# Feed-forward sums moved from POOL to DVE, and the next stage's first weights called for earlier

## The chip, the cores and the metric

The kernel runs on one core of a Trainium2 chip. The time is the device time of one execution, in microseconds (us); what is compared is the median of several executions. The engines are named as in the profile: PE (TensorE, matrix products; its weight loads are PEld), DVE (VectorE), ACT (ScalarE), POOL (GpSimd) and SP (SyncE, which issues most of the transfers from memory). Each engine runs its own instructions in order; a semaphore makes one wait for another.

## What is computed

A sequence of 512 tokens with 1024 features goes through two layers and a tail. Everything is in fp32.

```python
def _rmsnorm(x, gain):
    x32 = x.astype(jnp.float32)
    y = x32 * lax.rsqrt(jnp.mean(x32 * x32, axis=-1, keepdims=True) + NORM_EPS)
    return (y * gain).astype(x.dtype)

def _swiglu(x, w_gate, w_up, w_down):
    hid = jax.nn.silu(jnp.einsum('bsd,df->bsf', x, w_gate)) * jnp.einsum('bsd,df->bsf', x, w_up)
    return jnp.einsum('bsf,fd->bsd', hid, w_down)
```

Each of the two layers is a feed-forward stage (`ffn1`), a mixer (mLSTM, retention and gated delta side by side) and a second feed-forward stage (`ffn2`), each behind its own RMS norm and added to the residual stream `h`. The tail is a second mixer (a state-space part and a gated linear recurrence), a fifth feed-forward stage and a last norm. The change touches the five feed-forward stages, which are called here `ffn1_0`, `ffn2_0`, `ffn1_1`, `ffn2_1` and the last one.

## The kernel before, in words

**Data.** `h` is kept transposed, as eight tiles of 128 features by 512 tokens, `self.h[0]` to `self.h[7]` (in the order they are `h_77` to `h_84`). A product in fp32 is made of three: weight and input are both split in a high and a low half (ACT rounds the high half, DVE subtracts it to get the low half: `split` L260 and L261, `parts_of` L207 and L210), and PE adds high by high, high by low and low by high. A split weight of 1024 columns is `whi` and `wlo`; the parts of a quad are `wah/wal`, `wbh/wbl`, `wdh/wdl`.

**A feed-forward stage.** The gate and up weights are taken two by two: a *quad* is a block of 2 by 2 weight tiles, and one block of the output is made with seven products (named a to g) of sums of these weights with sums of the inputs, instead of eight. A quad with its seven products is called a pair here, as in the code; a gate pair and an up pair together give two tiles of hidden activations. A stage has 22 pairs, 20 of them loaded in full (100 in the kernel) and two from early weights. `load_quad` (L385 on) loads a quad: SP's `wsum` (L392), `wa` (L393) and `wrest` (L394), and a DMA issued by POOL that adds a second part of the quad into `wsum` in place (L395). `prepare` (L424 on) makes the weight sums that the seven products need, `wdh/wdl` from `ws = wsum + wrest` (L441), and the last ones from `wrest + ws` (L446). The sum at L441 is a POOL operation, kept in program order on POOL.

**The inputs.** `even` (L455 on) and `odd` (L473 on) make the input sums from two neighbouring tiles of `h`: `xe`, `xo` (scaled by the gain, on ACT), `n` and `t` (DVE), and their splits `bh/bl`, `nh/nl`, `th/tl`. `square` (L490) calls `squares` (L317): ACT squares a tile of `h` (L320), and POOL adds it to a running sum, each time into a new tile `sqa` (L324). The mixers and the last norm use `squares` too. `total` (L327) multiplies the sum with ones on PE to `nps` (L331), and `rsqrt` (L264) makes from it `R`, the scale of the norm, which is multiplied into the outputs of the products (`taken`, L511 on). So the products start before the norm is known.

**Order.** `items` writes out the order of a stage's products by hand; two are ahead of where their weights are made (`SPLITS` = 11 us of planned time) and loads twice as far (`LOADS` = 22). The instructions of each engine are then put in order by the Tile scheduler, by priorities and a model of time, within what the program allows. `wlo` of the sums for f and g, made from `wrest`, is the last to be ready in a pair.

**Early weights.** A stage's first two quads are loaded ahead in the stage before: `ahead` (L556) loads eight tiles `wr` (L406, 256 KB each) and makes their first sums `ws` (L409, DVE) and splits `weh/wel`. It is called by `nxt()`, a function that each stage is given: in `ffn` when it comes to the fifth of the last group's eight output products (`mm == 4`), in the first mixers at the third block of the output projection, in the second mixer at block 4. Before a mixer, `nxt()` only begins the stream of weights (`begin`, L226).

Of the kernel before, what the change touches and what calls it, by code (L numbers as in the profile page):

```python
# [11 lines left out]
AF = mybir.ActivationFunctionType  # L12
ALU = mybir.AluOpType
# [130 lines left out]
class Builder:  # L144
# [279 lines left out]
    def prepare(self, w, p):  # L424

        nc = self.nc
        if p in w.part:
            return
        if hasattr(w, "raw"):
            return self.prepare_early(w, p)  # L430
        lo, hi = slice(0, 512), slice(512, 1024)
        if p == "a":
            w.part["a"] = self.split(w.a11, "wa")
        elif p in "ce":
            t = self.parts_of(w.sums, late=True)
            w.part["e"], w.part["c"] = [x[:, lo] for x in t], [x[:, hi] for x in t]
        elif p == "b":
            w.part["b"] = self.split(w.rest[:, hi], "wb")
        elif p == "d":
            w.s2 = self.slot("ws")  # L440
            self.tc.keep_in_program_order(nc.gpsimd.tensor_tensor(w.s2, w.sums[:, lo], w.rest[:, lo], ALU.add))  # L441
            w.part["d"] = self.split(w.s2, "wd")
        else:
            self.prepare(w, "b")
            self.prepare(w, "d")
            nc.vector.tensor_tensor(w.rest[:, hi], w.rest[:, hi], w.s2, ALU.add)  # L446
            t = self.parts_of(w.rest)
            w.part["g"], w.part["f"] = [x[:, lo] for x in t], [x[:, hi] for x in t]
# [39 lines left out]
        self.split_to(tt, t)  # L488

    def square(self, v, k):  # L490
        v.acc = self.squares(k, v.acc)

    def matmuls(self, m, p, j, x, last):

# [75 lines left out]
    def ffn(self, gain, names, l, factor, nxt):  # L570
        nc = self.nc
# [8 lines left out]
        v = type("Normed", (), dict(gain=gain, xs=[], tmp={}, acc=None))  # L580
# [28 lines left out]
        sizes = [2 * (b - a) for a, b in zip((-1,) + ENDS, ENDS + (FB // 2 - 1,))]  # L609
# [7 lines left out]
        for c, it in enumerate(items):  # L617
            t = 0.0
            for d in range(c, len(items)):
                k, i, q = items[d][:3]  # L620
                if t > LOADS:
                    break
                if k == "p":
                    if pairs[i].w is None:
                        pairs[i].w = self.load_quad(pairs[i].key)
                    if t < SPLITS:
                        self.prepare(pairs[i].w, q)
                elif t < SPLITS:
                    for u in range(where[d] // UNIT, (where[d] + count(items[d]) - 1) // UNIT + 1):
                        self.load_unit(u)  # L630
                t += cost[d]
            if r is None and c >= (0 if start else 4):
                r = self.slot("R")
                self.rsqrt(r, self.total(v.acc), 1.0 / DM, self.slot)
                for m in pairs:
                    m.r = r
            if it[0] == "d":
                _, g, mm, ks, first, last = it
                if g == len(sizes) - 1 and mm == 4:
                    nxt()  # L640
                if first:
                    pds[mm] = self.ps("pd", tag=("mm", "mx")[mm % 2])
                self.mm3(pds[mm], (names[2], l, mm), (hids[g] if ks.stop is None else hids[g][:sizes[g] - 2])[ks if ks.stop is None else slice(None)], first=first, last=last)
                if last:
                    nc.vector.scalar_tensor_tensor(self.h[mm], pds[mm], factor, self.h[mm], ALU.mult, ALU.add)  # L645
                continue
            _, i, p = it
            m = pairs[i]
            self.product(m, p, v.xs)
            if p == "g" and i % 2 == 0:  # L650
                for o in m.o:
                    nc.scalar.activation(o, o, AF.Silu)
            elif p == "g":
                f = i // 2
                hid = hids[sum(f > e for e in ENDS)]
                for j, (g, u) in enumerate(zip(pairs[i - 1].o, m.o)):
                    nc.vector.tensor_tensor(g, g, u, ALU.mult)
                    hid.append((2 * f + j,) + self.split(g, "hid"))
# [98 lines left out]
    def mixer1(self, l, nxt):  # L757
        nc = self.nc
        if l == 0:
            self.ealog = self.const.tile([P, DEPTH + 1], F32, name="ealog")  # L760
            self.tc.keep_in_program_order(nc.scalar.activation(self.ealog, self.cols[:, COLS["alog"]:COLS["alog"] + DEPTH + 1], AF.Exp))
        xs, r, total = self.norm(f"mix_{l}")
        m = type("Mix", (), dict(l=l, xs=xs, r=r, y=[]))
        ps = self.proj(("small", l), xs)
        self.lockstep([self.rows1(m, ps), self.by_token(m, total), self.values(m)])
        self.queue = [self.retention(m), self.mlstm(m)]
        self.lockstep([self.delta(m, h) for h in range(GH)], STARTS, lambda i: int((i + 1) * RATE) - int(i * RATE))
        self.drain()
        for mm, pd in self.out_proj(("w_out", l), m.y, range(KB)):
            if mm == 2:  # L770
                nxt()
            nc.vector.tensor_tensor(self.h[mm], pd, self.h[mm], ALU.add)

    def out_proj(self, key, y, blocks, late=2, wave=4):
# [379 lines left out]
    def mixer2(self, after):  # L1154
        nc = self.nc
        xs, r, v, ps1 = self.norm_of_norm("final", "norm1")
# [15 lines left out]
        for g, d in enumerate(groups):  # L1172
            nxt = groups[g + 1] if g + 1 < SG else None
# [22 lines left out]
            nc.gpsimd.tensor_tensor(t, t, m.acc[j], ALU.add)  # L1196
            mix.append((j,) + self.split(t, "mix"))
        for j in range(KB):
            if j == 4:
                after()  # L1200
            ps = self.ps("pd")
            self.mm3(ps, ("w_out2", j), mix)
            nc.vector.scalar_tensor_tensor(self.h[j], ps, 0.5, self.h[j], ALU.mult, ALU.add)
# [456 lines left out]
```

## Time and profile before

| | us |
|---|---|
| median of 3 runs | 3453.12 (3452.86 to 3454.13) |
| the profiled execution, its own time | 3450.36 |
| its span, first to last instruction | 3448.2 |
| PE busy | 3197.3 (93%) |
| DVE busy | 2469.5 (72%) |
| ACT busy | 1557.1 (45%) |
| POOL busy | 663.4 (19%) |
| POOL, sums for d (L441), 100 | 161.0 |
| mean granted clock of PE | 0.971 |

The profile shows one execution. Its busy times say how much each engine had to do, its timeline when, and its waits which engine stood still and for whom. A line such as "PE pW L501 <- DVE wlo L210" says that PE stood still before a product at line 501 until DVE had finished a `wlo` at line 210. PE is the engine that is to be kept busy; idle time elsewhere matters only where PE waits for it in the end. The stages lie, by the first products of each, at about 0 (`ffn1_0`), 790 (`ffn2_0`), 1171 (`ffn1_1`), 1933 (`ffn2_1`) and 3077 us (the last).

### The profile page before, as it was taken

The numbers are of one execution on the slowest core, as the hardware profiler recorded it, in microseconds if no ns is written. First come the engines' busy times: TensorE is split into PE (matmuls) and PEld (weight loads), VectorE is DVE, ScalarE is ACT, GpSimd is POOL, SyncE is SP. The second block draws the span as 40 slices with busy tenths as digits, with TensorE's granted clock in tenths as the row PEclk, the third lists the DMA queues.
The fourth block names the chain that finished last, engine by engine and source line by source line (L and its number), as shares of the span: only waits on it lengthen the run. The fifth ranks groups of instructions, "written<-read, shape, count | busy, mean of one in ns | idle before, by whom it ended". The sixth has DMA issues, their size and how long they took to land.

```text
span 3448.2 us, 48282 instructions
## 1 busy us (share of the span) xinstructions
PE 3197.3 (93%) x18602; PEld 2755.7 (80%) x18602; DVE 2469.5 (72%) x4144; ACT 1557.1 (45%) x2607; POOL 663.4 (19%) x779
## 2 busy tenths in 40 slices
PE   5999999987999799999999799999999998999998
PEld 5988877777898698887777698887777777879887
DVE  6765778667685695677866686578788887568655
ACT  5443543335353453344334454355444366355334
POOL 2111124202111111112431211132111123121111
PEclk7999999998999899999999899999999999999999
DMA  5564222134554355433212346423333222345642
GB/s 147 137 169 133 84 94 75 45 98 109 145 138 129 113 139 155 135 95 101 72 55 70 108 132 162 132 80 107 92 97 105 83 80 79 116 124 140 163 132 79
DMA packets 142614, 383.53 MB, mean 111 GB/s; under 512 B 22320, under 2 KB 38832, under 8 KB 142384
## 3 DMA queue, kind: packets, MB, share of 16 engines
q1 hardware_dynamic: 127984, 328.02, 29.8%
q0 software_dynamic: 14400, 52.44, 9.5%
q8 instruction: 145, 2.38, 0.3%
q14 instruction: 85, 0.70, 0.1%
HBM read 376.99 MB, written 2.88 MB: 110 GB/s over the span
## 4 chain that ended last, share of the span: by engine, by line
PE 51%; DVE 24%; ACT 10%; issue 6%; DMA 5%; POOL 4%; SPq 0%; DVEq 0%; POOLq 0%; ACTq 0%
PE pd L248 7%; PE pd L250 7%; PE pd L249 7%; PE pX L501 7%; DVE wlo L210 6%; PE pW L501 3%; PE pj L250 3%; PE pj L249 3%; PE pj L248 3%; DMA wraw<-ws 2%; ACT whi L207 2%; DVE wbl L261 2%; PE pV L501 2%; DVE cacc L715 1%; DVE wrest L446 1%
## 5 line engine op out<-in xcount | busy, mean ns | idle before, releaser
L210 DVE TENSOR_TENSOR wlo<-wraw,whi 128x1024 fp32r<-128x1024 f32 x306 | 391.0, 1278 | 263.8 <-ACT whi L207 206.5
L207 ACT ACTIVATE whi<-wraw 128x1024 fp32r<-128x1024 f32 x306 | 322.4, 1054 | 461.0 <-DMA wraw<-ws 410.0
L249 PE MATMUL pd<-hidl,whi 128*128 128x512 f32 x880 | 347.0, 394 | 0.0
L250 PE MATMUL pd<-hidh,wlo 128*128 128x512 f32 x880 | 346.7, 394 | 0.0
L248 PE MATMUL pd<-hidh,whi 128*128 128x512 f32 x880 | 346.3, 394 | 0.0
L395 POOL DMA_DIRECT2D wsum<-wq x100 | 87.7, 877 | 1247.7 <-DMA wsum<-wq 902.5
L501 PE MATMUL pX<-tl,whi 128*128 128x256 f32 x800 | 224.7, 281 | 0.0
L501 PE MATMUL pX<-th,whi 128*128 128x256 f32 x800 | 224.7, 281 | 0.0
L501 PE MATMUL pX<-th,wlo 128*128 128x256 f32 x800 | 224.5, 281 | 0.0
L250 PE MATMUL pj<-x,wlo 128*128 128x512 f32 x476 | 191.8, 403 | 4.7 <-DVE wlo L210 4.7
L250 PEld LDWEIGHTS pd<-hidh,wlo 128*128 128x128 f32 x880 | 165.2, 188 | 38.6
L248 PEld LDWEIGHTS pd<-hidh,whi 128*128 128x128 f32 x880 | 165.3, 188 | 38.2
L249 PEld LDWEIGHTS pd<-hidl,whi 128*128 128x128 f32 x880 | 165.2, 188 | 38.0
L250 PE MATMUL pj<-xh,wlo 128*128 128x512 f32 x476 | 192.1, 404 | 3.3 <-DVE wlo L210 3.3
L248 PE MATMUL pj<-x,whi 128*128 128x512 f32 x476 | 192.6, 405 | 0.6 <-ACT whi L207 0.4
L248 PE MATMUL pj<-xh,whi 128*128 128x512 f32 x476 | 190.2, 400 | 3.1 <-ACT whi L207 3.1
L249 PE MATMUL pj<-x,whi 128*128 128x512 f32 x476 | 191.6, 403 | 0.0
L249 PE MATMUL pj<-xl,whi 128*128 128x512 f32 x476 | 189.3, 398 | 0.0
L441 POOL TENSOR_TENSOR ws<-wsum,wrest 128x512 f32<-128x512 f32 x100 | 161.0, 1610 | 119.4 <-DMA wsum<-wq 51.0
L645 DVE SCALAR_TENSOR_TENSOR h<-pd,h 128x512 f32<-128x512 f32 x120 | 82.4, 687 | 111.4 <-PE pd L250 111.3
L715 DVE SCALAR_TENSOR_TENSOR cacc<-cpad,cols,cacc 128x512 f32<-128x512 f32 x174 | 137.5, 790 | 28.0 <-ACT cacc L711 15.6
L501 PE MATMUL pW<-nh,wlo 128*128 128x256 f32 x400 | 117.2, 293 | 42.7 <-DVE wlo L210 42.7
(503 smaller groups left out, 9771.4 us busy)
## 6 DMA issues: line engine op xcount, KB each, us to landing
wraw<-ws SPq DMA_DIRECT2D x306, 512.0 KB
wsum<-wq SPq DMA_DIRECT2D x100, 512.0 KB
wrest<-wq SPq DMA_DIRECT2D x100, 512.0 KB
wsum<-wq POOLq DMA_DIRECT2D x100, 512.0 KB, 6.2
wa<-wq SPq DMA_DIRECT2D x100, 256.0 KB
wr<-wq SPq DMA_DIRECT2D x40, 256.0 KB
csb<-drow SPq DMA_DIRECT2D x32, 256.0 KB
bc<-drow SPq DMA_DIRECT2D x24, 256.0 KB
```

The lines of the kernel that those rows point to most:

```text
L207: ins = self.nc.scalar.activation(hi, src, AF.Copy)
L210: self.nc.vector.tensor_tensor(lo, src, hi.bitcast(F32), ALU.subtract)
L248: nc.tensor.matmul(ps, lhsT=wh, rhs=xh, start=st, stop=False)
L249: nc.tensor.matmul(ps, lhsT=wh, rhs=xl, start=False, stop=False)
L250: nc.tensor.matmul(ps, lhsT=wl, rhs=xh, start=False, stop=en)
L261: self.nc.vector.tensor_tensor(lo, src, hi.bitcast(F32), ALU.subtract)
L395: nc.gpsimd.dma_start(w.sums, src[:, 512:1536], accum_op=ALU.add)
L441: self.tc.keep_in_program_order(nc.gpsimd.tensor_tensor(w.s2, w.sums[:, lo], w.rest[:, lo], ALU.add))
L446: nc.vector.tensor_tensor(w.rest[:, hi], w.rest[:, hi], w.s2, ALU.add)
L501: self.nc.tensor.matmul(m.ps[bank][:, 0:HT], lhsT=a[:, j * P:(j + 1) * P], rhs=b, start=p in "acb" and j + i == 0, stop=last and i == 2, s ...
L645: nc.vector.scalar_tensor_tensor(self.h[mm], pds[mm], factor, self.h[mm], ALU.mult, ALU.add)
L715: nc.vector.scalar_tensor_tensor(acc, x[:, 1 + j:1 + j + S], w(j), acc, ALU.mult, ALU.add)
```

## The change

Three things are changed. The sum `ws = wsum + wrest` for product d is issued to DVE instead of POOL (it keeps its place in program order, now on DVE). In the feed-forward stages the running sum of squares is added on DVE, in place into the first square's tile, instead of on POOL into new tiles; the norms of the mixers and the last norm keep `squares`. And `nxt()` is called earlier: in `ffn` before the first output product of the last group, in the first mixers before the output projection, in the second mixer at block 1.

```diff
--- before.py
+++ after.py
@@ -438,7 +438,7 @@
             w.part["b"] = self.split(w.rest[:, hi], "wb")
         elif p == "d":
             w.s2 = self.slot("ws")
-            self.tc.keep_in_program_order(nc.gpsimd.tensor_tensor(w.s2, w.sums[:, lo], w.rest[:, lo], ALU.add))
+            self.tc.keep_in_program_order(nc.vector.tensor_tensor(w.s2, w.sums[:, lo], w.rest[:, lo], ALU.add))
             w.part["d"] = self.split(w.s2, "wd")
         else:
             self.prepare(w, "b")
@@ -488,7 +488,13 @@
         self.split_to(tt, t)
 
     def square(self, v, k):
-        v.acc = self.squares(k, v.acc)
+
+        sq = self.slot("sq")
+        self.nc.scalar.activation(sq, self.h[k], AF.Square)
+        if v.acc is None:
+            v.acc = sq
+        else:
+            self.nc.vector.tensor_tensor(v.acc, v.acc, sq, ALU.add)
 
     def matmuls(self, m, p, j, x, last):
 
@@ -636,7 +642,7 @@
                     m.r = r
             if it[0] == "d":
                 _, g, mm, ks, first, last = it
-                if g == len(sizes) - 1 and mm == 4:
+                if g == len(sizes) - 1 and mm == 0 and first:
                     nxt()
                 if first:
                     pds[mm] = self.ps("pd", tag=("mm", "mx")[mm % 2])
@@ -766,9 +772,8 @@
         self.queue = [self.retention(m), self.mlstm(m)]
         self.lockstep([self.delta(m, h) for h in range(GH)], STARTS, lambda i: int((i + 1) * RATE) - int(i * RATE))
         self.drain()
+        nxt()
         for mm, pd in self.out_proj(("w_out", l), m.y, range(KB)):
-            if mm == 2:
-                nxt()
             nc.vector.tensor_tensor(self.h[mm], pd, self.h[mm], ALU.add)
 
     def out_proj(self, key, y, blocks, late=2, wave=4):
@@ -1196,7 +1201,7 @@
             nc.gpsimd.tensor_tensor(t, t, m.acc[j], ALU.add)
             mix.append((j,) + self.split(t, "mix"))
         for j in range(KB):
-            if j == 4:
+            if j == 1:
                 after()
             ps = self.ps("pd")
             self.mm3(ps, ("w_out2", j), mix)
```

100 + 35 additions leave POOL and come to DVE; the other engines keep their instructions, in an order that differs locally. Three places show how.

The end of `ffn2_0`, on ACT, where the last output products' weights are split (`whi<-wraw`), the early weights of `ffn1_1` are split (`weh`), the hidden activations are split (`hidh`), and the first `h` of `ffn1_1` is scaled (`xe<-h_77`). Before:

```order
L652 ACTIVATE o<-o 128x512 x2
L207 ACTIVATE whi<-wraw 128x1024 x3
L260 ACTIVATE hidh<-o 128x512 x2
L207 ACTIVATE whi<-wraw 128x1024 x2
L260 ACTIVATE weh<-wr 128x512 x2
L260 ACTIVATE weh<-ws 128x512 x2
L466 ACTIVATE xe<-h_77,cols 128x512
L452 ACTIVATE bh<-xe 128x256
L452 ACTIVATE nh<-n 128x256
```

With the change:

```order
L658 ACTIVATE o<-o 128x512 x2
L207 ACTIVATE whi<-wraw 128x1024
L260 ACTIVATE weh<-wr 128x512 x2
L260 ACTIVATE weh<-ws 128x512
L207 ACTIVATE whi<-wraw 128x1024
L260 ACTIVATE weh<-ws 128x512
L260 ACTIVATE hidh<-o 128x512
L207 ACTIVATE whi<-wraw 128x1024
L260 ACTIVATE hidh<-o 128x512
L466 ACTIVATE xe<-h_77,cols 128x512
L207 ACTIVATE whi<-wraw 128x1024
L452 ACTIVATE bh<-xe 128x256
```

Two to four `whi<-wraw` and the `hidh` that stood ahead of the four `weh` now stand behind them, and `xe<-h_77` no longer waits for all of them. On SP the eight `wr` loads go out ahead of the last four `wraw` loads. At the ends of the mixers the orders show no such move.

The opening of `ffn2_0`, on DVE, from the last input sum `t` to `rv`, the first step of the norm's scale (`wel` and `ws` are early weights, `wal` and `wlo` belong to the first full quad). Before:

```order
L487 SCALAR_TENSOR_TENSOR t<-n,xo 128x256
L453 TENSOR_TENSOR tl<-t,th 128x512
L409 TENSOR_TENSOR ws<-wr 128x512
L261 TENSOR_TENSOR wel<-ws,weh 128x512
L261 TENSOR_TENSOR wal<-wa,wah 128x512
L409 TENSOR_TENSOR ws<-wr,ws 128x512
L210 TENSOR_TENSOR wlo<-wsum,whi 128x1024
L261 TENSOR_TENSOR wel<-ws,weh 128x512
L527 TENSOR_TENSOR oq<-pX,oq 128x256
L261 TENSOR_TENSOR wel<-wr,weh 128x512
L268 TENSOR_SCALAR rv<-nps 128x512
```

With the change:

```order
L487 SCALAR_TENSOR_TENSOR t<-n,xo 128x256
L453 TENSOR_TENSOR tl<-t,th 128x512
L409 TENSOR_TENSOR ws<-wr 128x512
L497 TENSOR_TENSOR sq<-sq 128x512
L261 TENSOR_TENSOR wel<-ws,weh 128x512
L261 TENSOR_TENSOR wal<-wa,wah 128x512
L409 TENSOR_TENSOR ws<-wr,ws 128x512
L210 TENSOR_TENSOR wlo<-wsum,whi 128x1024
L261 TENSOR_TENSOR wel<-ws,weh 128x512
L261 TENSOR_TENSOR wel<-wr,weh 128x512
L268 TENSOR_SCALAR rv<-nps 128x512
```

The last addition of squares, `sq<-sq`, now stands here between two steps of the early weights, and `oq<-pX,oq` comes after `rv`.

A pair of quads in the same stage, on DVE, from the low half of one sum to that of the next (`o` are outputs of products). Before:

```order
L210 TENSOR_TENSOR wlo<-wsum,whi 128x1024
L534 SCALAR_TENSOR_TENSOR o<-oq,R 128x256
L261 TENSOR_TENSOR wbl<-wrest,wbh 128x512
L522 TENSOR_TENSOR o<-pV,snap 128x256
L446 TENSOR_TENSOR wrest<-wrest,ws 128x512
L529 TENSOR_TENSOR o<-pW,snap 128x256
L261 TENSOR_TENSOR wdl<-ws,wdh 128x512
L530 TENSOR_TENSOR o<-o,R 128x512
L210 TENSOR_TENSOR wlo<-wrest,whi 128x1024
```

With the change:

```order
L210 TENSOR_TENSOR wlo<-wsum,whi 128x1024
L540 SCALAR_TENSOR_TENSOR o<-oq,R 128x256
L261 TENSOR_TENSOR wbl<-wrest,wbh 128x512
L528 TENSOR_TENSOR o<-pV,snap 128x256
L441 TENSOR_TENSOR ws<-wsum,wrest 128x512
L446 TENSOR_TENSOR wrest<-wrest,ws 128x512
L535 TENSOR_TENSOR o<-pW,snap 128x256
L261 TENSOR_TENSOR wdl<-ws,wdh 128x512
L536 TENSOR_TENSOR o<-o,R 128x512
L210 TENSOR_TENSOR wlo<-wrest,whi 128x1024
```

The sum `ws<-wsum,wrest` has come in behind `o<-pV,snap`, directly ahead of the addition that uses it.

## Rows read from the trace of the kernel before

**Rows 1.** The page: busy time of each engine, and the chain that ended last.

```profile
PE 3197.3 (93%) x18602; PEld 2755.7 (80%) x18602; DVE 2469.5 (72%) x4144; ACT 1557.1 (45%) x2607; POOL 663.4 (19%) x779
...
PE 51%; DVE 24%; ACT 10%; issue 6%; DMA 5%; POOL 4%; SPq 0%; DVEq 0%; POOLq 0%; ACTq 0%
```

**Rows 2.** Waits, whole span: waiter <- releaser: us in total, times, longest.

```profile
POOL ws L441 <- DMA wsum<-wq: 51.0, 12, 5.0
...
PE pW L501 <- DVE wlo L210: 42.7, 39, 2.4
...
DVE o L522 <- PE pV L501: 5.9, 14, 0.7
```

**Rows 3.** Groups by form, POOL then DVE: busy us, mean ns | idle before.

```profile
L441 POOL TENSOR_TENSOR ws<-wsum,wrest 128x512 f32<-128x512 f32 x100 | 161.0, 1610 | 119.4 <-DMA wsum<-wq 51.0 <-DVE R L274 32.8 <-DVE wel L261 10.4
...
L210 DVE TENSOR_TENSOR wlo<-wrest,whi 128x1024 fp32r<-128x1024 f32 x100 | 121.6, 1216 | 6.5 <-ACT whi L207 6.4
L261 DVE TENSOR_TENSOR wbl<-wrest,wbh 128x512 fp32r<-128x512 f32 x100 | 99.5, 995 | 41.2 <-ACT wbh L260 41.1
L446 DVE TENSOR_TENSOR wrest<-wrest,ws 128x512 f32<-128x512 f32 x100 | 84.5, 845 | 0.3
```

**Rows 4.** Tile `wbl`, its DVE line: duration in ns, minimum/median/maximum.

```profile
L261 DVE TENSOR_TENSOR wbl<-wrest,wbh x100: 675/685/2618, 74.3 to 3390.4; 128x512 fp32r<-128x512 f32 x100
```

**Rows 5.** Timeline, a pair late in `ffn2_0`: start, us, engine, operation [idle before].

```profile
1100.16 2.47 DVE L261 TENSOR_TENSOR wbl<-wrest,wbh 128x512 fp32r<-128x512 f32 x1 [1.03 <-ACT wbh L260]
...
1100.47 1.59 POOL L441 TENSOR_TENSOR ws<-wsum,wrest 128x512 f32<-128x512 f32 x1
...
1102.88 0.68 DVE L446 TENSOR_TENSOR wrest<-wrest,ws 128x512 f32<-128x512 f32 x1
...
1105.08 0.39 PE L501 MATMUL pW<-nh,wlo 128*128 128x256 f32 x1 [0.91 <-DVE wlo L210]
```

**Rows 6.** Timeline, opening of `ffn1_0`.

```profile
32.72 0.43 DVE L483 SCALAR_TENSOR_TENSOR n<-n,xo 128x256 f32<-128x256 f32 x1
...
36.38 0.75 DVE L522 TENSOR_TENSOR o<-pV,snap 128x256 f32<-128x256 f32 x2
...
38.20 9.69 POOL L324 TENSOR_TENSOR sqa<-sqa,sq 128x512 f32<-128x512 f32 x6
...
47.84 0.90 POOL L395 DMA_DIRECT2D wsum<-wq  x1
47.95 0.69 DVE L261 TENSOR_TENSOR wel<-ws,weh 128x512 fp32r<-128x512 f32 x1 [1.17 <-POOL sqa L324]
...
47.95 2.08 PE L331 MATMUL nps<-sqa,cst 128*128 128x512 f32 x2 [12.61 <-POOL sqa L324]
```

**Rows 7.** Timeline, opening of `ffn2_0`.

```profile
792.62 1.05 DVE L483 SCALAR_TENSOR_TENSOR n<-n,xo 128x256 f32<-128x256 f32 x1 [0.71 <-ACT xo L482]
...
806.90 2.08 PE L331 MATMUL nps<-sqa,cst 128*128 128x512 f32 x2 [4.60 <-POOL sqa L324]
...
813.85 1.69 POOL L441 TENSOR_TENSOR ws<-wsum,wrest 128x512 f32<-128x512 f32 x1 [1.30 <-DVE wal L261]
...
814.29 2.33 DVE L210 TENSOR_TENSOR wlo<-wsum,whi 128x1024 fp32r<-128x1024 f32 x1
...
824.87 0.38 PE L501 MATMUL pX<-th,weh 128*128 128x256 f32 x1 [2.73 <-ACT weh L260]
```

**Rows 8.** Timeline, end of `ffn2_0`; beginning of `ffn1_1`.

```profile
1139.92 1.06 ACT L207 ACTIVATE whi<-wraw 128x1024 fp32r<-128x1024 f32 x1 [2.84 <-DMA wraw<-ws]
...
1142.43 0.69 DVE L645 SCALAR_TENSOR_TENSOR h<-pd,h 128x512 f32<-128x512 f32 x1 [4.01 <-PE pd L250]
...
1151.67 0.71 ACT L466 ACTIVATE xe<-h,cols 128x512 f32<-128x512 f32 x1
```

**Rows 9.** Windows: busy us of each engine, granted clock, DMA share, GB/s.

```profile
60.00:390.00 330.00, 314.48 (x2177) 291.81 (x2177) 231.82 (x343) 147.71 (x235) 43.81 (x37) 0.99 0.50 133
1088.00:1105.50 17.50, 15.86 (x132) 15.44 (x131) 13.40 (x19) 8.44 (x14) 4.39 (x4) 1.00 0.70 157
```

## The prediction

> **What bounds the kernel now.** Four views were read, in this order. The page first: TensorE (PE) is busy 93% of the span and holds 51% of the chain that ended last; VectorE (DVE) is busy 72% and holds 24%; GpSimd (POOL) is busy 19% and holds 4% [rows 1]. So only time in which PE stands still can be won, and a part of that time is set by DVE. The waits come next: PE waits 39 times, 42.7 us in all, for `wlo`, the low half of a weight that DVE makes just before the products f [rows 2]. This is the repeated cost inside the feed-forward stages. The third view is the timeline of one such pair (a quad with its seven products). DVE's `wbl` starts at 1100.16, POOL's sum for d (L441) runs from 1100.47 to 1102.06, and `wbl` takes 2.47 us instead of its median 0.685 [rows 4, 5]. Behind it on DVE stand `o<-pV,snap`, `wrest<-wrest,ws` at 1102.88, ACT's `whi`, DVE's `wlo`, and PE starts late at 1105.08 after 0.91 us. The reader is to see that a POOL sum of 1.59 us costs DVE about as much as it costs POOL. The last view is the opening of a stage: PE waits 12.61 us in the first one and 4.60 us in `ffn2_0` for POOL's running sum of squares [rows 6, 7].
>
> **Part one: 100 sums for d go to DVE.** Removed from POOL: 100 operations of 1.61 us [rows 3]. Added to DVE: 100 operations of the same shape as `wrest`'s add and `wbl`, so 0.68 us each (the median of [rows 4]), 68 us in all, in a queue that is 232 of 330 us busy in such a stage [rows 9]. Given back: `wbl` averages 0.995 and `wrest`'s add 0.845 where 0.685 is the median of the shape, which is 31 + 16 = 47 us over 200 operations [rows 3, 4]; other operations that meet a sum (the `wlo` of 2.33 us in [rows 7] is one) come on top. DVE's total is thus about even, but the hold is not spread evenly: it sits in the pairs where PE waits. In the shown pair, without the hold, `wbl` ends at 1100.85, `o` at 1101.2, the new sum at 1101.9, and `wrest`'s add starts then instead of at 1102.88. That is 1.0 us earlier and covers the whole 0.91 us on PE. With the hold of that pair (1.8 us) less the added 0.68, the net is 1.1 us; with a smaller hold of 1.3 us it would be 0.6. I take 0.64 us for each of the 39 waits: **-25 us**. The bounds are -42.7 (all of the waits) and 0 (nothing, the rival below). The 61 pairs in which PE does not wait pay 0.68 us out of the time that DVE is idle; if that cover were gone they would cost 61 x 0.68 = 41 us. On POOL, the accumulating DMAs of later quads (L395) keep their order and lose a neighbour in the queue; nothing there gets later.
>
> The Trainium skill, page SBUF — State Buffer, section Who interferes with whom, says that a DVE operation with two SBUF inputs and a GpSimd operation that reads SBUF exclude each other, and that the one that starts first holds the shared interface while the other waits it out. The shown pair agrees with the full exclusion, but not with the order: `wbl` has the earlier start and was the one held. By the order rule alone the hold would not come from the sum, the steady gain would be 0, and the time that of rival C.
>
> **Part two: 35 adds of squares go to DVE.** In `ffn1_0` all eight squares come together. POOL's last six adds take 9.69 us, to 47.89, and PE's `nps` waits for them to 47.95 [rows 6]. On DVE, after `o` at 37.13, there now stand four adds, one weight sum, two adds, one `wel` and the last add: nine operations of 0.68, to 43.3. That is **-4.6 us**; bounds -6 (nothing held, closer spacing) and -2 (ACT's squares come later than DVE can use them). The DMA at 47.84 that stood behind the adds on POOL goes out earlier too.
>
> In the other four stages (`ffn2_0`, `ffn1_1`, `ffn2_1`, and the last one) each add follows its square as it comes. Two operations `n<-n,xo` in the interval are held, 1.05 us [rows 7] against 0.43 where POOL stands still [rows 6], so 1.2 come back. The last add takes 0.68 in place of POOL's 1.6 (9.69 / 6), but one weight sum of 0.68 stands ahead of it now: -0.2. The inserted adds stand behind `tl`, where DVE next waits for ACT; I charge 0.2 for them. That is -1.2 us for each start, **-4.8 us**; bounds -10 (the adds free, all holds gone, 2.4 each) and +5 (two adds of 0.68 in the way at each, nothing back). Then R, the scale of the norm: the `wlo` at 814.29 took 2.33 us under the sum at 813.85 [rows 7] where 1.22 is the mean of its form [rows 3]. `rv`, the first step of R, stands behind it; in the new order no sum for d stands ahead of `rv`. PE waits 2.73 us at 824.87 behind R [rows 7]. -1.1 us for each of four starts: **-4.4 us**, bounds -10.9 and 0.
>
> **Part three: the next stage's early weights.** The order shows that only one of the places really changes: the end of `ffn2_0`. Before, `xe`, the first operation of the next stage on ACT, runs at 1151.67 although its `h` is ready at 1143.1 [rows 8]: it stood behind four `weh` that waited for their weights. Now they stand ahead of the last four `whi<-wraw`. Up to 8 us of the ACT and DVE chain that PE waits for at the opening of `ffn1_1` can start earlier. I take **-5 us**: the queue of `whi<-wraw` between them takes some of it. Bounds -8 and +13: the eight loads of 256 KB now go out ahead of the last four weight loads, and 2.1 MB at the 157 GB/s of a full stretch are 13 us [rows 9]; the `whi` at 1139.92 waited 2.84 us for its load already, so there is no slack to hide it [rows 8]. I take the gain, because the last loads were queued early and PE has the earlier products to do. In the mixers the call moves, the queues do not: 0.
>
> **Sum.** -25 - 4.6 - 4.8 - 4.4 - 5 = -43.8 us against the profiled execution's own 3450.4, so 3406.6. The median of the runs shown is 2.8 us above that execution, hence **3409 us**.
>
> **Rivals.** (A) *DVE becomes the bound: slower.* The hold comes from something else, such as the descriptor work of L395, and the 0.68 us land on PE in every pair: +68 us, less the 18.8 of the openings and early weights, gives 3502. For it: DVE is the second engine of the chain [rows 1]. Against it: at 47.95 a `wel` runs 0.69 us under an L395, unheld [rows 6], and DVE waited for PE before `o<-pV` only 14 times, 5.9 us [rows 2], so DVE's own backlog is what the return shortens. It decides from 0.19 us per pair on (18.8 us over 100).
>
> (B) *The wait moves along.* POOL waited 12 times, 51.0 us, for quad loads before a sum [rows 2]. DVE is in order, so splits for PE now queue behind that wait. If all of it shows, 3460, at the edge of slower. Against it: `wrest`'s add stands right behind and needed the same sum.
>
> (C) *Nothing in the steady stages*: hold and added sum cancel. Only -18.8 remains: 3434. For it: 68 us added against 47 counted back. The Trainium skill, page Perfetto Trace Analysis, section Optimizing Scalar/DVE Operations, says the same of these two engines: as they share a read port, moving work from one to the other might not help. The pair in [rows 5] speaks against it.
>
> (D) *The early loads stall the end of `ffn2_0`*: +13 in place of -5, 3427.
>
> **How the numbers follow.** Forecast 0.60, C 0.15, D 0.11, A 0.08, B 0.06. Runs of this kernel tell 0.2% (7 us) from no change. The forecast, C and D are faster by more, less 0.03 for their upper tails: 0.83. B is half no change, half slower: with the tails 0.06 same; A and half of B: 0.11 slower. The range runs from 3380 (steady waits all gone and the openings near their lower bounds, about 70 us) to 3440 (C and some of its openings lost); A, B and the tails outside are just under 0.2.
>
> **What would show it.** Right: `wbl` near 0.69 and `wrest`'s add near 0.68 us on average; the wait of PE for `wlo` under 20 us; `nps` of the first stage near 43 us instead of 48; POOL near 450 us busy (663 less 161 for the sums and some 50 for the adds); DVE's busy time within 20 us of before. Wrong: DVE 60 us busier with `wlo` waits of PE at 40 or more (A or C), DVE waiting for `wsum` loads ahead of splits (B), or ACT's `whi<-wraw` waiting over 6 us near 1140 (D).

## The result, and the profile after

The changed kernel takes 3367.0 us (median of 4 runs, 3364.3 to 3370.8) where the kernel before takes 3453.0: a ratio of 0.9751, 95% interval 0.9735 to 0.9768, 86 us less. The direction was forecast; the size was not, and the range of 3380 to 3440 does not hold it.

The page of the changed kernel, its busy times and its chain, against [rows 1]:

```profile
PE 3177.6 (94%) x18602; PEld 2745.7 (82%) x18602; DVE 2438.4 (72%) x4279; ACT 1554.5 (46%) x2607; POOL 471.4 (14%) x644
...
PE 66%; DVE 17%; ACT 8%; issue 4%; POOL 3%; DMA 2%; SPq 0%; DVEq 0%; ACTq 0%; POOLq 0%
```

PE has the same 18602 products and holds 66% of the chain instead of 51%; DVE's share falls from 24% to 17%, though DVE has 135 operations more. Its busy time is 31 us less: 92 us of additions came (68.1 at L441, 24.1 at L497), so some 123 us of other time went. POOL is down to 471 us, near the 450 forecast.

The waits of PE that are now longest (waiter, releaser: us in all, times, longest):

```profile
PE pX L507 <- ACT bh L452: 23.4, 6, 5.5
PE pX L507 <- ACT weh L260: 20.7, 6, 8.5
PE nps L331 <- DVE sq L497: 14.0, 4, 3.8
```

The wait for `wlo`, 42.7 us and PE's longest before [rows 2], is 0.6 us now, and the one for the squares' sum, in all five stages together, 14.0. The groups of DVE by form, for [rows 3] and [rows 4]:

```profile
L210 DVE TENSOR_TENSOR wlo<-wrest,whi 128x1024 fp32r<-128x1024 f32 x100 | 121.7, 1217 | 0.0
...
L261 DVE TENSOR_TENSOR wbl<-wrest,wbh 128x512 fp32r<-128x512 f32 x100 | 68.6, 686 | 30.8 <-ACT wbh L260 30.8
...
L446 DVE TENSOR_TENSOR wrest<-wrest,ws 128x512 f32<-128x512 f32 x100 | 68.4, 684 | 0.3
...
L441 DVE TENSOR_TENSOR ws<-wsum,wrest 128x512 f32<-128x512 f32 x100 | 68.1, 681 | 0.0
...
L497 DVE TENSOR_TENSOR sq<-sq 128x512 f32<-128x512 f32 x35 | 24.1, 687 | 1.8 <-ACT sq L493 0.5
```

`wbl` and `wrest`'s add now average 686 and 684 ns, their length alone. They are not the only ones. Three more forms, in the kernel before:

```profile
L210 DVE TENSOR_TENSOR wlo<-wsum,whi 128x1024 fp32r<-128x1024 f32 x100 | 132.2, 1322 | 25.3 <-ACT whi L207 25.2
...
L530 DVE TENSOR_TENSOR o<-o,R 128x512 f32<-128x512 f32 x110 | 82.9, 753 | 0.7
...
L261 DVE TENSOR_TENSOR wal<-wa,wah 128x512 fp32r<-128x512 f32 x100 | 80.7, 807 | 22.5 <-ACT wah L260 22.0
```

and with the change:

```profile
L210 DVE TENSOR_TENSOR wlo<-wsum,whi 128x1024 fp32r<-128x1024 f32 x100 | 122.4, 1224 | 79.8 <-PE pd L249 47.0 <-ACT whi L207 17.4 <-ACT wbh L260 8.9
...
L536 DVE TENSOR_TENSOR o<-o,R 128x512 f32<-128x512 f32 x110 | 75.2, 683 | 0.2
...
L261 DVE TENSOR_TENSOR wal<-wa,wah 128x512 fp32r<-128x512 f32 x100 | 68.5, 685 | 7.8 <-ACT wah L260 7.1
```

A pair late in `ffn2_0`, DVE alone, for [rows 5]:

```profile
1071.78 0.69 DVE L261 TENSOR_TENSOR wbl<-wrest,wbh 128x512 fp32r<-128x512 f32 x1 [0.90 <-ACT wbh L260]
1072.38 0.42 DVE L528 TENSOR_TENSOR o<-pV,snap 128x256 f32<-128x256 f32 x1
1072.72 0.68 DVE L441 TENSOR_TENSOR ws<-wsum,wrest 128x512 f32<-128x512 f32 x1
1073.32 0.68 DVE L446 TENSOR_TENSOR wrest<-wrest,ws 128x512 f32<-128x512 f32 x1
1073.92 0.42 DVE L535 TENSOR_TENSOR o<-pW,snap 128x256 f32<-128x256 f32 x1
1074.59 1.23 DVE L210 TENSOR_TENSOR wlo<-wsum,whi 128x1024 fp32r<-128x1024 f32 x1 [0.25 <-PE pX L507]
1075.73 0.68 DVE L261 TENSOR_TENSOR wdl<-ws,wdh 128x512 fp32r<-128x512 f32 x1
1076.33 1.22 DVE L210 TENSOR_TENSOR wlo<-wrest,whi 128x1024 fp32r<-128x1024 f32 x1
```

`wbl`, `o`, the new sum and `wrest`'s add follow each other without a hole, as worked out ahead: 1.5 us from the start of `wbl` to that of `wrest`'s add, where it was 2.7. And the opening of `ffn1_0`, for [rows 6]:

```profile
36.40 0.75 DVE L528 TENSOR_TENSOR o<-pV,snap 128x256 f32<-128x256 f32 x2
...
37.07 2.27 DVE L497 TENSOR_TENSOR sq<-sq 128x512 f32<-128x512 f32 x3
39.86 0.69 DVE L497 TENSOR_TENSOR sq<-sq 128x512 f32<-128x512 f32 x1 [0.52 <-ACT sq L493]
...
40.51 0.87 POOL L395 DMA_DIRECT2D wsum<-wq  x1 [19.05 <-DMA wsum<-wq]
41.07 1.48 DVE L497 TENSOR_TENSOR sq<-sq 128x512 f32<-128x512 f32 x2
...
43.07 0.68 DVE L497 TENSOR_TENSOR sq<-sq 128x512 f32<-128x512 f32 x1
...
44.02 1.91 PE L331 MATMUL nps<-sq,cst 128*128 128x512 f32 x2
```

PE's `nps` starts at 44.02 instead of 47.95, and POOL's DMA, no longer behind the adds, at 40.51 instead of 47.84.

Where the 84 us between the two profiled spans (3448.2 and 3364.3) lie is read from two kinds of marks in each trace, the second `nps` product of a stage and the end of its last `h<-pd`. "Opening" is from the last `h` of the stage before to `nps`, "body" from there to the stage's own last `h`. Differences to the kernel before, in us:

| | openings, five in order | bodies, five in order | mixers | all |
|---|---|---|---|---|
| the change | -4.1, -2.4, -5.2, -2.8, -0.3 | -11.4, -13.6, -16.5, -15.0, -10.8 | -1.4 | -83.4 |
| only the 100 sums | +0.3, 0, 0, 0, +0.1 | -11.5, -10.2, -13.9, -12.0, -11.1 | -1.9 | -60.3 |
| only the squares | -4.2, -2.6, -1.5, -2.8, -0.3 | +3.0, +0.1, -1.9, -2.1, +3.7 | -4.4 | -12.9 |
| only the earlier weights | -0.1, 0, -3.6, 0, 0 | -0.1, +2.6, -2.6, -3.1, +2.9 | -4.2 | -8.1 |
| sums and squares | -4.3, -2.4, -1.3, -3.0, -0.8 | -10.3, -13.6, -16.8, -14.6, -11.4 | -7.9 | -86.1 |

A single execution differs from the next by a few us, above all in the mixers, so the last column is only good to that. Second profiles of the change and of sums and squares repeat the openings within 0.3 us and the bodies within 0.6 and 2.1. Where POOL's sums remain, the bodies can scatter more: with only the earlier weights the last stage, behind which there is nothing to load early, differs by 2.9.

### The profile page after: what moved, and what is told of

Its sections match the earlier page's. It is cut to its first block, busy times and chain, and to the rows that moved or that the text cites. A ratio compares the mean times of both kernels' runs of the same rounds, so it can differ in the third digit from the quotient of the medians.

```text
span 3364.3 us, 48101 instructions
## 1 busy us (share of the span) xinstructions
PE 3177.6 (94%) x18602; PEld 2745.7 (82%) x18602; DVE 2438.4 (72%) x4279; ACT 1554.5 (46%) x2607; POOL 471.4 (14%) x644
## 4 chain that ended last, share of the span: by engine, by line
PE 66%; DVE 17%; ACT 8%; issue 4%; POOL 3%; DMA 2%; SPq 0%; DVEq 0%; ACTq 0%; POOLq 0%
PE pX L507 15%; PE pd L250 8%; PE pd L248 8%; PE pd L249 8%; PE pW L507 7%; PE pV L507 4%; PE pj L250 3%; PE pj L249 3%; PE pj L248 3%; DVE wlo L210 3%; DVE cacc L721 1%; PE pt L678 1%; PE pt L679 1%; PE pt L680 1%; DMA bc<-drow 1%
## 5 line engine op out<-in xcount | busy, mean ns | idle before, releaser
L395 POOL DMA_DIRECT2D wsum<-wq x100 | 86.6, 866 | 1623.6 <-DMA wsum<-wq 1028.2
L210 DVE TENSOR_TENSOR wlo<-wsum,whi 128x1024 fp32r<-128x1024 f32 x100 | 122.4, 1224 | 79.8 <-PE pd L249 47.0
L507 PEld LDWEIGHTS pX<-th,whi 128*128 128x128 f32 x800 | 150.8, 189 | 3.5 <-DVE oq L533 3.5
```

The source lines that it names most:

```text
L210: self.nc.vector.tensor_tensor(lo, src, hi.bitcast(F32), ALU.subtract)
L395: nc.gpsimd.dma_start(w.sums, src[:, 512:1536], accum_op=ALU.add)
L507: self.nc.tensor.matmul(m.ps[bank][:, 0:HT], lhsT=a[:, j * P:(j + 1) * P], rhs=b, start=p in "acb" and j + i == 0, stop=last and i == 2, s ...
```

## The experiments

### The parts alone

Each of the three parts was made alone in the kernel before, and the first two together. Only the sums for d:

```diff
-            self.tc.keep_in_program_order(nc.gpsimd.tensor_tensor(w.s2, w.sums[:, lo], w.rest[:, lo], ALU.add))
+            self.tc.keep_in_program_order(nc.vector.tensor_tensor(w.s2, w.sums[:, lo], w.rest[:, lo], ALU.add))
```

> Only the 100 sums for d go to DVE. If nearly all of the steady gain is theirs: 3453 less some 62, 3391 (3385 to 3398), PE's waits for wlo at nearly 0, the openings as before (nps of the first stage near 48 us). Rival, that the steady stages gained through the squares or the earlier weights too (the whole order moved): 3410 to 3425, with half of the 42.7 us of waits still there.

Measured: 0.9831 of before (0.9816 to 0.9845), 58 us. The page of this kernel:

```profile
PE 3184.2 (94%) x18602; PEld 2751.8 (81%) x18602; DVE 2436.1 (72%) x4244; ACT 1556.2 (46%) x2607; POOL 522.2 (15%) x679
```

The waits of PE for `wlo` are 0.4 us in all, the openings stand as before. Five bodies give 10 to 14 us each. So the sums carry two thirds of the gain by themselves; the first theory holds.

Only the squares:

```diff
-        v.acc = self.squares(k, v.acc)
+        sq = self.slot("sq")
+        self.nc.scalar.activation(sq, self.h[k], AF.Square)
+        if v.acc is None:
+            v.acc = sq
+        else:
+            self.nc.vector.tensor_tensor(v.acc, v.acc, sq, ALU.add)
```

> Only the 35 adds of squares go to DVE. If the openings gain by themselves: 4 us in the first stage and about 2.5 us in each of ffn2_0, ffn1_1 and ffn2_1, nothing in the last: 3453 less 11, 3442 (3438 to 3446), waits for wlo still 40 us or more. Rival, that the openings gained because the sums for d had left POOL's queue: under 5 us, 3448 or more.

Measured: 0.9967 (0.9956 to 0.9978), 11 us. The openings gain what they gain in the whole change, the first 4.2 us and the next three 2.6, 1.5 and 2.8; only `ffn1_1` gains more in the whole change (5.2), and that is the third part. Two waits of PE in this kernel:

```profile
PE pW L507 <- DVE wlo L210: 41.6, 36, 2.7
...
PE nps L331 <- DVE sq L497: 13.9, 4, 3.8
```

The wait for `wlo` is still there, that for the squares is 13.9 us in the feed-forward stages (32.7 before, with those of the other norms). The openings gained by themselves.

Only the earlier call for weights:

```diff
-                if g == len(sizes) - 1 and mm == 4:
+                if g == len(sizes) - 1 and mm == 0 and first:
                     nxt()
...
+        nxt()
         for mm, pd in self.out_proj(("w_out", l), m.y, range(KB)):
-            if mm == 2:
-                nxt()
...
-            if j == 4:
+            if j == 1:
                 after()
```

> Only the earlier call for the next stage's weights. If it makes the second half of the gain at the opening of ffn1_1: -2 to -5 us there and nothing elsewhere, 3449 (3446 to 3452). Rival, that it does nothing that can be measured: 3452 to 3455. Rival, that the early loads delay the last products of ffn2_0: 3456 or more.

Measured: 0.9993 (0.9981 to 1.0005), no difference. ACT's timeline of this kernel, the row that was at 1151.67 [rows 8]:

```profile
1146.68 0.72 ACT L466 ACTIVATE xe<-h,cols 128x512 f32<-128x512 f32 x1 [3.43 <-DVE h L645]
```

`xe` is 5 us earlier, and now waits for its `h`, which is made 3.5 us later than before (1146.6 instead of 1143.1). The opening of `ffn1_1` gains 3.6 us. The 2.6 us that the body of `ffn2_0` has lost are not the price of it, for 2.1 of them were lost by the sixteenth `h<-pd`, at 1085.2, and the first early load is issued at 1118.8: the end of the stage, from there to its last `h<-pd`, takes 81.5 us instead of 81.0. So some 3 to 4 us are gained at one place, which the times of whole executions (2 us less, between 7 less and 2 more) cannot tell from nothing.

The first two parts together, without the third, ran twice, the second time on one chip with the changed kernel itself.

> The change without the earlier weights. If the parts add up: 3367 plus 2 to 5 us, 3371 (3368 to 3374). Rival, that the order of the stage ends matters more: 3378 or more.

> The changed kernel again, as the measure for the other three on the same chip: about 0.975 of before.

> The change without the earlier weights, on the chip on which the change itself runs. If the earlier weights only trade the end of ffn2_0 for the opening of ffn1_1: within 4 us of the changed kernel. Rival, that they give my 5 us: 4 to 8 us slower.

Measured: 0.9767 (0.9750 to 0.9784) at first; on the common chip 0.9756 (3368.4 us) against 0.9746 (3365.8 us) of the change, intervals that overlap. In the profiles the earlier weights show in one place, the opening of `ffn1_1`, which gains 5.2 us with them and 1.3 without; the body of `ffn2_0` gains 13.6 either way. The first two parts give 11 to 14 us more together than one by one (0.0233 and 0.0244 off, where 0.0169 and 0.0033 make 0.0202), though each of these is known only to some 5 us: in the table the bodies gain 67 us together, where the sums alone give 59 and the squares alone cost 3. A part of it is PE's wait for `th,weh` behind R: 10.8 us before, 9.9 with the sums, 8.0 with the squares, 5.6 with both. The 8 us that both gain over the sums alone lie at the beginning of the bodies: from `nps` to the first `h<-pd`, `ffn2_0`, `ffn1_1` and `ffn2_1` together take 310 us before and with the sums, 305 with the squares, 302 with both. The squares alone lose some 7 us in the rest of the bodies, about what bodies with sums on POOL scatter by. More than that is not explained.

### Hold or lateness

A sum on POOL could cost in two ways: it holds DVE while it runs, or it comes late, since it takes 1.6 us and stands in POOL's queue. Two kernels separate them. The first puts the load back on POOL without its result: to the changed kernel, 100 additions of constants in the old place, which nobody reads (`dz` is a spare tile).

```diff
             self.tc.keep_in_program_order(nc.vector.tensor_tensor(w.s2, w.sums[:, lo], w.rest[:, lo], ALU.add))
...
+            f = lambda i: self.cst[:, i:i + 4, :].rearrange("p a b -> p (a b)")
+            self.tc.keep_in_program_order(nc.gpsimd.tensor_tensor(self.dz, f(0), f(4), ALU.add))
```

> The changed kernel plus 100 additions of constants on POOL, of the same shape and in the old place of the sums in POOL's order, whose result nobody reads. If the cost of before was the hold of DVE by a running POOL sum: DVE's wbl and its neighbours average 0.8 us or more again, waits for wlo come back in part, 12 to 45 us slower than the changed kernel (3380 to 3412). Rival, that it was the late arrival of the sum (POOL's queue and its 1.61 us): no more than 5 us slower, 3372 or less.

Measured: 1.0016 of before (1.0005 to 1.0027), that is 3459 us: the whole gain of the change is gone, 91 us at 0.9751. The expectation for the hold named 12 to 45 us, so its direction came true and its size did not. Two waits of PE, the page, and three rows of the timeline of a pair:

```profile
PE pW L511 <- DVE wlo L210: 50.1, 47, 2.1
...
PE pX L511 <- DVE oq L537: 12.2, 8, 2.3
```

```profile
PE 3199.0 (93%) x18602; PEld 2755.0 (80%) x18602; DVE 2543.6 (74%) x4279; ACT 1554.3 (45%) x2607; POOL 612.3 (18%) x744
```

```profile
1007.44 1.60 POOL L445 TENSOR_TENSOR dz<-cst 128x512 f32<-128x512 f32 x1
...
1007.64 1.95 DVE L441 TENSOR_TENSOR ws<-wsum,wrest 128x512 f32<-128x512 f32 x1
...
1009.52 0.68 DVE L450 TENSOR_TENSOR wrest<-wrest,ws 128x512 f32<-128x512 f32 x1
```

DVE is busy 105 us more than in the changed kernel with the same operations. In the timeline the sum on DVE starts 0.2 us after POOL's addition and takes 1.95 us instead of 0.68; it ends 0.55 us after POOL's 1009.04. Nobody needs POOL's result, so lateness is out. The hold alone is enough.

Which operations are held can be counted in the trace of the kernel before. Of 118 DVE operations with both inputs in SBUF that run beside one of the 100 sums, 74 are more than 0.15 us longer than others of their form; of 38 with an input from PSUM (`o<-pV`, `o<-pW`, `oq<-pX` and such), none is longer by more than 0.02 us.

The second leaves the hold and takes the lateness away: in the kernel before, the sum stays on POOL and is issued a step earlier, with the split of `wsum`.

```diff
             t = self.parts_of(w.sums, late=True)
+            self.early_sum(w)
...
-            w.s2 = self.slot("ws")
-            self.tc.keep_in_program_order(nc.gpsimd.tensor_tensor(w.s2, w.sums[:, lo], w.rest[:, lo], ALU.add))
+            self.early_sum(w)
...
+    def early_sum(self, w):
+        if getattr(w, "s2", None) is None:
+            nc, lo = self.nc, slice(0, 512)
+            w.s2 = self.slot("ws")
+            self.tc.keep_in_program_order(nc.gpsimd.tensor_tensor(w.s2, w.sums[:, lo], w.rest[:, lo], ALU.add))
```

> The kernel before, with the sum for d still on POOL but issued one step earlier, when the sums for e and c are split. If the late arrival was the cost: the waits for wlo fall under 15 us and 30 to 55 us are won, 3392 to 3417. Rival, that the hold was the cost: it only meets other DVE operations, waits for wlo stay over 25 us, 3432 to 3450.

Measured: 0.9978 (0.9967 to 0.9990), 8 us. Three waits of PE, and two groups of DVE:

```profile
PE pX L507 <- ACT snap L523: 19.4, 23, 1.5
...
PE pW L507 <- DVE wlo L210: 12.6, 24, 1.5
PE pX L507 <- DVE oq L533: 12.2, 18, 1.0
```

```profile
L210 DVE TENSOR_TENSOR wlo<-wsum,whi 128x1024 fp32r<-128x1024 f32 x100 | 143.6, 1436 | 68.5 <-ACT whi L207 34.7 <-ACT wbh L260 33.9
...
L261 DVE TENSOR_TENSOR wbl<-wrest,wbh 128x512 fp32r<-128x512 f32 x100 | 83.4, 834 | 62.6 <-ACT wbh L260 58.9 <-DMA wa<-wq 3.6
```

The wait for `wlo` did fall to 12.6 us, as the lateness would have it, but PE now waits for `snap` (7.4 us before) and `oq` instead, and `wlo<-wsum` averages 1436 ns where its length alone is 1224. The hold has met other operations of the chain: DVE is busy 2458.3 us in all, only 11 less than before. The time, not the one wait, decides: the expectation of 3432 to 3450 for the hold is the one that holds, though not by the row that it named.

### What POOL has to do to hold DVE

> The changed kernel plus 100 writes of a constant on POOL (128x512, nothing read), where the additions of constants cost 92 us. If the hold comes from what POOL reads, as the Trainium skill, page SBUF - State Buffer, section Who interferes with whom, has it: within 8 us of the changed kernel (3367 to 3375). Rival, that any POOL work at that place holds DVE or delays POOL's transfers: 3390 or more.

Against the kernel with the additions of constants:

```diff
-            self.tc.keep_in_program_order(nc.gpsimd.tensor_tensor(self.dz, f(0), f(4), ALU.add))
+            self.tc.keep_in_program_order(nc.gpsimd.memset(self.dz, 1.0))
```

Measured: 3362.4 us, 0.9727 (0.9707 to 0.9746). That is no slower than the changed kernel (0.9735 to 0.9768 on another chip; the two intervals overlap). The group of the writes on POOL, and the page:

```profile
L444 POOL MEMSET dz<- 128x512 f32 x100 | 81.2, 812 | 0.9
```

```profile
PE 3172.6 (95%) x18602; PEld 2743.5 (82%) x18602; DVE 2439.3 (73%) x4279; ACT 1555.0 (46%) x2607; POOL 526.0 (16%) x744
```

100 writes of 0.81 us in the same place, and DVE's busy time is that of the changed kernel (2438.4): of the 154 operations with both inputs in SBUF that run beside a write, none is held by more than 0.01 us. Such work on POOL, its place and the delay of its transfers cost nothing that can be measured. The additions differ from the writes in that they read SBUF. The Trainium skill, page SBUF — State Buffer, section Who interferes with whom, says this: an operation of DVE with two SBUF inputs meets a GpSimd operation that reads, not one that only writes. The trace agrees: 105 us of DVE's time beside the additions against none beside the writes, and no hold where one of DVE's inputs came from PSUM.

> The changed kernel plus 100 additions of constants on POOL of half the width (128x256). If a hold first uses up the slack of its pair (about 0.4 us, as the 68 us of added DVE work that cost some 22 us say) and only the rest reaches PE: 10 to 35 us slower than the changed kernel, 3377 to 3402. Rival, that a hold costs in proportion to its length: half of 92, 3408 to 3418.

Again against the kernel with the additions of full width:

```diff
-            self.tc.keep_in_program_order(nc.gpsimd.tensor_tensor(self.dz, f(0), f(4), ALU.add))
+            self.tc.keep_in_program_order(nc.gpsimd.tensor_tensor(self.dz[:, lo.start:256], f(0)[:, 0:256], f(4)[:, 0:256], ALU.add))
```

Measured: 3401.0 us, 39 us above the kernel with the writes on the same chip. The page:

```profile
PE 3190.5 (94%) x18602; PEld 2750.7 (81%) x18602; DVE 2499.8 (74%) x4279; ACT 1553.6 (46%) x2607; POOL 556.7 (16%) x744
```

The additions of half width take 1.05 us each, little more than a write of a constant (0.81), and DVE is busy 61 us more than with the writes. So it is not the time that POOL is busy that holds DVE. 3401.0 us lies just inside the interval of the theory with a slack (3377 to 3402); by the kernel with the writes, on the same chip, the 39 us are just above its 35, and under the rival's half of 92. Per microsecond of DVE's added time it is 39 / 61 = 0.64 us, where the full width costs 91 / 105 = 0.87: the first part of a hold is cheaper than the rest.

### What an added sum on DVE costs

> The changed kernel plus a second addition (of constants, result unread) on DVE behind each sum: another 68 us of DVE work in the same place. If the added 0.68 us lie in DVE's slack, as the vanished waits say: at most 10 us slower, 3377 or less. Rival, that DVE was at its limit with the change (my 0.64 us per wait, half eaten by the added sum): waits for wlo come back with 20 us or more, 3387 to 3435.

```diff
             self.tc.keep_in_program_order(nc.vector.tensor_tensor(w.s2, w.sums[:, lo], w.rest[:, lo], ALU.add))
...
+            self.tc.keep_in_program_order(nc.vector.tensor_tensor(self.dz, f(0), f(4), ALU.add))
```

Measured: 3388.4 us, 0.9816 (0.9799 to 0.9834), 22 us above the change at 0.9751. The page, and the longest new wait of PE:

```profile
PE 3191.4 (94%) x18602; PEld 2749.2 (81%) x18602; DVE 2492.4 (73%) x4379; ACT 1552.6 (46%) x2607; POOL 471.2 (14%) x644
```

```profile
PE pX L511 <- DVE oq L537: 11.1, 26, 1.0
```

68 us more of DVE's work cost a third of that. Neither expectation holds whole: it is more than the 10 us of the first, and the time is at the lower edge of the rival's (3387 to 3435), but the waits for `wlo` are 4.3 us and not 20. With twice as much:

> The changed kernel plus two additions of constants on DVE behind each sum, 1.36 us per pair, about as long as a hold. If a hold costs what the DVE time in it costs, and the pair's slack is 0.4 us: about 0.9 us per pair, 70 to 105 us slower than the changed kernel. Rival, that DVE time behind the sum is cheaper than a hold and a hold does more than take DVE's time: 30 to 60 us slower.

```diff
+            self.tc.keep_in_program_order(nc.vector.tensor_tensor(self.dz, f(0), f(4), ALU.add))
+            self.tc.keep_in_program_order(nc.vector.tensor_tensor(self.dz, f(0), f(4), ALU.add))
```

Measured: 3433.9 us, 68 us above the changed kernel on the same chip (3365.8). That is a little under the first interval and above the second. The first 68 us of DVE's work cost 22, the next 68 cost 46: as if there were a slack in each pair that the first one uses up for the most part. But 136 us of it cost 68, while 105 us of holds cost 91. So a microsecond of hold is dearer than one of work behind the sum. A hold meets whichever operation comes, and some pairs not at all, which is a reason, but it was not tried with holds of equal length in every pair; this stays open.

### Attempts at a faster kernel

> The changed kernel with the norm's sum on PE two products later in four openings. If PE's 14 us of waits for nps are only its place in PE's order: 6 to 12 us faster than the changed kernel, 3355 to 3361. Rival, that the scale R then comes late and PE waits there: within 3 us or slower.

```diff
-            if r is None and c >= (0 if start else 4):
+            if r is None and c >= (0 if start else 6):
```

Measured: 3374.7 us, 0.9777 (0.9761 to 0.9793), no gain, rather some us lost. Waits of PE:

```profile
PE pW L507 <- ACT weh L260: 29.8, 11, 7.5
PE pV L507 <- ACT weh L260: 16.9, 5, 4.7
...
PE nps L331 <- DVE sq L497: 10.0, 4, 3.1
```

`nps` is waited for 10.0 instead of 14.0 us; the products that now stand ahead of it wait for their `weh` instead, 29.8 us where `pW` waited 11.2. `nps` starts no earlier and no later than in the change, and from there to the first `h<-pd` it is some 3 us longer in the three middle stages. By these waits the opening is bound by the chain of splits on ACT and DVE, wherever `nps` stands.

> The changed kernel with only the 34 adds of squares of the mixers' norms and the last norm moved to DVE too. If their hold or their 1.5 us each delays the norms: 3 to 10 us faster, 3357 to 3364. Rival, no difference that can be measured: 3364 to 3370.

> The changed kernel with the 34 other adds of squares and 32 products and adds of the second mixer moved from POOL to DVE too. If holds cost there as in the feed-forward stages (13 us under squares, some 20 under the others): 10 to 30 us faster, 3337 to 3357. Rival, that PE does not wait for DVE there: within 6 us of the changed kernel, or slower where DVE is the late engine.

> The changed kernel with the 34 other adds of squares and 32 operations of the second mixer on DVE, on the same chip as the changed kernel. If their holds reach PE: 6 to 15 us faster. Rival: within 5 us.

```diff
-        nc.gpsimd.tensor_tensor(new, acc, sq, ALU.add)
+        nc.vector.tensor_tensor(new, acc, sq, ALU.add)
...
-            nc.gpsimd.tensor_tensor(xt, xt, yo, ALU.add)
+            nc.vector.tensor_tensor(xt, xt, yo, ALU.add)
...
-            nc.gpsimd.tensor_tensor(ig, ig, th, ALU.mult)
+            nc.vector.tensor_tensor(ig, ig, th, ALU.mult)
...
-            nc.gpsimd.tensor_tensor(w, w, t, ALU.mult)
+            nc.vector.tensor_tensor(w, w, t, ALU.mult)
```

The first line alone gives 3360.8 us (0.9724), all four 3359.1 (0.9723), on a chip on which the changed kernel did not run, but the one with the writes did (3362.4 us). On a common chip all four give 3358.7 us (3358.3 to 3363.8) against 3365.8 (3360.8 to 3367.2): 7 us, with intervals of the ratio that overlap (0.9721 to 0.9747, 0.9733 to 0.9760). That is within the expected 6 to 15 us; whether it is a gain at all is not shown.

## Why the prediction was right and wrong

**The 100 sums: right mechanism, wrong size.** The step that failed is "I take 0.64 us for each of the 39 waits: -25 us". The part alone measured -58 us, and the waits did not shrink, they went: from 42.7 us to 0.4. Three things are in the difference. First, the term set the added 0.68 us against the returned hold in full. dve_dummy shows what one more such sum costs in the changed kernel: 0.22 us per pair, not 0.68. Second, only the holds of `wbl` and of `wrest`'s add were counted, 47 us [rows 3]. With the lengths of after for seven forms (`wal` 807 to 685 ns, `wlo<-wsum` 1322 to 1224, `o<-o,R` 753 to 683, `hidl` 732 to 683, `o<-oq,R` 471 to 414, `wbl` and `wrest` as above) it is 88 us; by DVE's busy time it is 101 (2469.5 before and 68 added, where 2436.1 was measured). pool_dummy prices a microsecond of such a hold at 91 / 105 = 0.87. An estimate from these runs, 88 or 101 x 0.87 - 22, is 55 to 66 us. Third, the bound of -42.7 us was no bound. It is the sum of PE's rows of idle time; but a product is shown 0.28 us long and the next one usually starts 0.12 us after it, so the beginning of each stall is counted as busy. Counted by the starts of the products at L501, the time above the usual 0.118 us from one to the next is 172 us before and 113 with the sums alone. These 59 us are what the part gave, and the 39 waits for `wlo` are 49 of them.

**The squares: right; R: right in size, wrong in cause.** -4.6 us forecast for `ffn1_0`, -4.2 measured; `nps` was expected near 43.3 and came at 44.02, as ACT's squares held DVE up once for 0.52 us. The other four openings were forecast at -1.2 each, -4.8 in all; b_only gives -7.2 (-2.6, -1.5, -2.8, -0.3), within the bounds. R: -4.4 forecast, and PE's wait for `th,weh` fell by 5.2, but not from the sums alone as the step had it: they gave 0.9, the squares alone 2.8. That the size came out is luck. (The 1.22 us of this step is the mean of `wlo<-wrest` in [rows 3], while the held operation is a `wlo<-wsum`; unheld, that one takes 1224 ns, so nothing hangs on it.) What the sum of the parts left out is that sums and squares give 11 to 14 us more together.

**The earlier weights: as forecast where they act, too small for the times.** -5 us forecast; the opening of `ffn1_1` gains 3.6 in c_only, and 5.2 in the change where it gains 1.3 without this part. In whole executions it is 2 us alone and 2.5 on top of the other two parts, neither clear of the noise. Rival D, the stall at the end of `ffn2_0`, hardly shows: from the sixteenth `h<-pd` to the last it takes 81.5 us in c_only against 81.0, and 78.8 in the change against 78.9 without this part.

**The rivals.** A (DVE becomes the bound) falls in both of its steps: with all 100 DMAs of L395 still issued on POOL, `wbl` averages its length alone, and dve_dummy shows that a sum more on DVE costs a third of its length. B (the wait for loads moves to DVE) does not show: L441 has no idle time in front of it on DVE. C (hold and added sum cancel) took the Trainium skill's page Perfetto Trace Analysis, section Optimizing Scalar/DVE Operations, at its word: moving work between these two might not help as they share a port. Here the sums and squares won 80 to 84 us, in the direction from POOL to DVE, because the hold cost DVE more than the work: 161 us of POOL's reading sums cost DVE 88 to 101, and the same sums cost DVE 68 us of its own. The order rule of the Trainium skill, page SBUF — State Buffer, section Who interferes with whom, that the first to issue keeps the port and the other waits, stays undecided: of the 74 held operations of before, 40 are shown as starting more than 0.1 us after POOL's sum, as the rule has it, 15 within 0.1 us and 19 ahead of it, like the `wbl` of [rows 5]. No run here shows how the shown start and the issue are related.

## What to carry to other kernels

When DVE is on the critical path, an addition of two SBUF inputs on POOL is not free for being on an idle engine: sum the difference between mean and shortest duration over all of DVE's forms, and compare it with what the operation would cost on DVE. Price the two sides apart, the hold and the added work, since here a microsecond of hold cost 0.87 us (0.64 with half the width) and the first 0.68 us of added work in a pair a third of its length. And the idle rows of PE understate what its waits cost: with the sums alone they fell by 46 us in the quads' products, and the time from start to start by 59.

## What was not expected

That 100 additions on POOL which nobody reads cost 91 us, as much as the whole change had won, while 100 writes in their place cost nothing that can be measured. And that the time follows the hold, not the wait that it shows up in: with the sum issued earlier on POOL, PE's wait for `wlo` fell from 42.7 to 12.6 us and the kernel gained 8.
